# Row factors of eleven RMS norms: from a column of sums to a full-width product

## The chip, the cores and the metric

The kernel runs on one core of one Trainium2 chip. A core has a matrix engine (PE, TensorE), a vector engine (DVE), an activation engine (ACT), a slower general engine (POOL) and a queue that issues DMAs (SP). The engines run side by side, each takes its own instructions in order, and they wait for each other by semaphores. On-chip memory has 128 partitions; PE adds up its products in eight PSUM banks of 128x512 fp32.

The metric is the device time of one launch in microseconds (us). Lower is better. Runs of the kernel before: 2305.17, 2305.32 and 2305.44 us, median 2305.32.

## The reference, cut to what matters

Two layers over 512 tokens of width 1024. Each layer has four residual steps, and each step begins with a norm over the features of a token:

```python
def rmsnorm(x, g):
    xf = x.astype(jnp.float32)
    y = xf * lax.rsqrt(jnp.mean(xf * xf, axis=-1, keepdims=True) + RMS_EPS)
    return (y * g.astype(jnp.float32)).astype(x.dtype)

def swiglu(x, w_gu, w_down):
    g, u = jnp.split(x @ w_gu, 2, axis=-1)
    return (jax.nn.silu(g) * u) @ w_down

for i in range(DEPTH):                                            # DEPTH = 2
    h = h + 0.5 * swiglu(rmsnorm(h, ffn1_norm[i]), ...)
    hn = rmsnorm(h, mix_norm[i])
    h = h + (ssd_mixer(hn, ...) if i == 0 else neighbourhood_attention(hn, ...))
    h = h + 0.5 * swiglu(rmsnorm(h, ffn2_norm[i]), ...)
    gate = jax.nn.sigmoid(rmsnorm(h, ple_norm[i]) @ ple_w_gate[i])
    h = h + gate * rmsnorm(p[i] @ ple_w_proj[i], ple_post_norm[i])
```

The SSD mixer has one more norm, over its 2048 inner features, ahead of its output matrix. That makes eleven norms whose row factor, 1/sqrt(mean square + eps) of each token, is computed by the code that is changed here: two times (first FFN, mixer, second FFN, projection of `p`, gate), and the one inside the SSD. The norms of the attention's queries and keys have code of their own and stay.

## The kernel before, in words

**Layout and precision.** The stream `h` lies feature-major: eight tiles of 128 features by 512 tokens. A token is a column, so a norm's sum over features runs over the partitions and over the eight tiles. Nearly every matrix product is made of three fp32r products (fp32r is the rounded fp32 format that PE multiplies in one pass): high part by high part, high by low, low by high. Weights arrive by DMA as fp32 (`load_unit`), ACT casts them to the high part `wh` (L221, `split_raw`), DVE subtracts to get the low part `wl` (L223). There are three buffers of each, and `unit()` hands out the next pair. `gemm` issues the three products of every block (L278, L281, L282). In the FFNs most of the gate and up matrices run as a seven-product scheme over blocks with 256 columns (L508 to L510).

**The norm.** While a step writes `h`, it splits every tile by the norm's gain (L306, L307) and adds up squares: ACT squares (L328), POOL or, for the last tile, DVE adds into one 128x512 tile `acc` (L332). The products that follow run on the gained but unscaled tiles; the row factor is multiplied in where a result leaves PSUM, so it may come later than the first products. It is made in two steps:

- `begin`: PE sums `acc` over the partitions, four fp32 products with one column each (L346; every fp32 product stands as two records in the trace), so that the 512 sums lie as 128x4. DVE scales, adds eps (L349) and takes the inverse square root of the 128x4 tile by an integer seed and three Newton steps (`newton_rsqrt`, L313 to L319: eleven instructions).
- `end`: PE spreads the 128x4 factors to all partitions as 128x512, four fp32 products with the identity (L356), and ACT copies them from PSUM into a tile `rt` (L359).

`end` is written some products after `begin`. In an FFN the point for `begin` is `mid()`, inside the first pair of gate and up products; `end` comes after four blocks of the next product. In the SSD (`ssd`) `begin` follows the first product and `end` five blocks of the next; right behind `end`, DVE scales all eight tiles (L681, L687) and splits them (L304). In the attention (`keys`) and the gate (`ple`) the points lie in the same way within the first two or three products. After `begin`, an FFN calls `ahead(norm)`: the next four preparations of weights (sums and differences of weight blocks, L243 to L248, and splits), which on DVE are queued behind the instruction that the norm has left as `ss.last`.

**Order.** The kernel is written for a planner that follows the code's order as a priority, simulates the engines and issues on each engine the first instruction that is ready, so the order in the trace can differ from that of the code; `tc.issue_after` and `tc.keep_in_program_order` tie down single places. Tiles come from pools with a fixed number of buffers: `sq` (squares and their sum) 4, `rt` 3, PSUM banks `px` 3 and `mm` 5.

**Function tables.** ACT evaluates Silu, Tanh, Exp and Ln from a table that it has loaded; the trace shows each load as ACT_TABLE_LOAD. Casts, copies and squares run with whichever table is loaded. Before the change there are seven loads in the run.

Of the kernel before, what the change touches and what calls it, by code (L numbers as in the profile page):

```python
# [8 lines left out]
F32R = mybir.dt.float32r  # L9
I32 = mybir.dt.int32  # L10
AF = mybir.ActivationFunctionType
ALU = mybir.AluOpType
AX = mybir.AxisListType

P = 128
T = 512
D = 1024
# [8 lines left out]
EPS = 1e-6  # L26
NH = 32
NG = 8
NC = T // P
# [41 lines left out]
def trunk(ctx, tc, A, out):  # L71
    nc = tc.nc
    v, s, g, te, sy = nc.vector, nc.scalar, nc.gpsimd, nc.tensor, nc.sync


    cp = ctx.enter_context(tc.tile_pool(name="cp", bufs=1))
# [10 lines left out]
    def nm(t):  # L87
        uid[0] += 1
        return f"{t}{uid[0]}"

    def sm(shape, dt=F32):
        return sp.tile([P] + list(shape), dt, name=nm("sm"), tag="sm", bufs=12)

    def slot(tag, bufs):
        return lambda dt=F32: bp.tile([P, T], dt, name=nm(tag), tag=tag, bufs=bufs)

    hs, t2, sc, sq = slot("hs", 8), slot("t2", 7), slot("sc", 15), slot("sq", 4)

    def md(dt=F32):
        return bp.tile([P, 2, T], dt, name=nm("md"), tag="md", bufs=24)  # L100
# [4 lines left out]
    def rt():  # L105
        return bp.tile([P, T], F32, name=nm("rt"), tag="rt", bufs=3)

    def bank(tag, bufs):
        return ps.tile([P, T], F32, name=nm("ps"), tag=tag, bufs=bufs)

    mm_bank = lambda: bank("mm", 5)
    px_bank = lambda: bank("px", 3)
# [4 lines left out]
    msk = cp.tile([P, M_N], F32, name="msk")  # L117
    ones_d = cp.tile([P, P], F32, name="ones_d")
    v.memset(ones_d, 1.0 / D)

    idle = ps.tile([P, T], F32, name="idle", tag="px", bufs=3)
    for _ in range(14):
# [2 lines left out]
    ident = msk[:, M_ID:M_ID + P]  # L125
# [16 lines left out]
    stop = A.get("stage", 4 * DEPTH)  # L142
# [168 lines left out]
    def newton_rsqrt(m, y, a):  # L311

        v.tensor_scalar(out=y.bitcast(I32), in0=m.bitcast(I32), scalar1=1, scalar2=None, op0=ALU.arith_shift_right)  # L313
        v.tensor_scalar(out=y.bitcast(I32), in0=y.bitcast(I32), scalar1=-1, scalar2=0x5F3759DF,
                        op0=ALU.mult, op1=ALU.add)
        for _ in range(3):
            v.tensor_mul(out=a, in0=y, in1=y)
            v.scalar_tensor_tensor(out=a, in0=a, scalar=-0.5, in1=m, op0=ALU.mult, op1=ALU.mult)
            last = v.scalar_tensor_tensor(out=y, in0=a, scalar=1.5, in1=y, op0=ALU.add, op1=ALU.mult)  # L319
        return last  # L320

    class SumSq:
# [8 lines left out]
            else:  # L331
                (v if fast else g).tensor_add(out=self.acc, in0=self.acc, in1=q)  # L332

        def rsqrt(self, scale=1.0, eps=EPS):
            pt = px_bank()
            te.matmul(out=pt, lhsT=ones_d, rhs=self.acc, start=True, stop=True)
            m, a, y = sc(), sc(), rt()
            v.tensor_scalar(out=m, in0=pt, scalar1=scale, scalar2=eps, op0=ALU.mult, op1=ALU.add)
            newton_rsqrt(m, y, a)
            return y  # L340

        def begin(self, scale=1.0, eps=EPS):

            pt = px_bank()
            for c in range(NC):
                te.matmul(out=pt[:, c:c + 1], lhsT=self.acc[:, c * P:(c + 1) * P], rhs=ones_d[:, :1],  # L346
                          start=True, stop=True)
            m, a, self.y = sm([NC]), sm([NC]), sm([NC])
            v.tensor_scalar(out=m, in0=pt[:, :NC], scalar1=scale, scalar2=eps, op0=ALU.mult, op1=ALU.add)  # L349
            self.last = newton_rsqrt(m, self.y, a)  # L350

        def end(self):

            pt = px_bank()
            for c in range(NC):
                te.matmul(out=pt[:, c * P:(c + 1) * P], lhsT=self.y[:, c:c + 1].to_broadcast([P, P]), rhs=ident,  # L356
                          start=True, stop=True)
            r = rt()
            s.copy(out=r, in_=pt)  # L359
            return r  # L360

    class Norm:

# [13 lines left out]

        def count(self, k, fast=False):
            self.ss.add(h[k], fast=fast or k == KD - 1)

        def factor(self):
            return self.ss.rsqrt()

        def begin(self, half=False):
            if half:
# [1065 lines left out]
    for i in range(stop):  # L1451
        l, w = divmod(i, 4)
        last = i == stop - 1
        m = None if last else Norm(gains[i + 1], (lambda: md(F32R)) if w == 2 else xa)
# [112 lines left out]
```

## Time and profile before

| | us |
|---|---|
| median of 3 runs | 2305.32 |
| the profiled execution | 2305.77 |
| its span, first to last instruction | 2304.0 |
| PE busy in it | 2292.0 |
| DVE busy in it | 1826.6 |
| ACT busy in it | 1179.0 |
| POOL busy in it | 323.7 |
| mean granted clock of PE | 1.000 |

All times in the profile are of one execution, counted from the first instruction. A row of the order of time gives start and duration in us, engine, line, operation, tile written and tiles read, and how often; in brackets stands the idle time of the engine ahead of it and what ended it. A matmul's duration reaches to its modelled end, and matmuls overlap; what one costs is read from the starts of its neighbours. A row of groups ends in busy time and mean ns of one, then the idle time ahead of the group. A row of waits reads: who waited, for whom, us in total, times, longest. A row of the chain is start, duration, what.

### The profile page before, as it was taken

The page shows a single profiled execution, that of the slowest core. Times are in us where ns is not written, and L with a number is a line of the kernel's source. Part 1 is how long each engine was busy: PE and PEld are TensorE (multiplying, and loading weights), DVE is VectorE, ACT ScalarE, POOL GpSimd, SP SyncE. Part 2 cuts the span into 40 slices and gives each one's busy share as a digit, 9 for nine tenths or more (in the row PEclk, how much of TensorE's full clock was granted, in tenths as well). Part 3 has the DMA queues.
Part 4 walks back from the last instruction along what each step waited for, and adds up shares of the span by engine and source line. Part 5 has one row for each costly group of instructions (what it writes and reads, how often), then busy time and mean ns, then how long its engine had stood idle before and what let it go on. Part 6 is the DMA issues. An engine that isn't in the chain of part 4 may idle for free.

```text
span 2304.0 us, 35426 instructions
## 1 busy us (share of the span) xinstructions
PE 2292.0 (99%) x13732; PEld 2025.5 (88%) x13732; DVE 1826.6 (79%) x2621; ACT 1179.0 (51%) x2038; POOL 323.7 (14%) x261
## 2 busy tenths in 40 slices
PE   9999999999999999999999999999999999999999
PEld 8899998888888888999998889999878888999987
DVE  7878878888788958987885897787578859887866
ACT  5433445877676864444445444444446745444452
POOL 0000001355555641000003100000110010000020
PEclk9999999999999999999999999999999999999999
DMA  5323323444444543333223233232557732333222
GB/s 185 116 83 106 110 73 130 164 155 138 146 140 151 188 158 119 106 101 106 94 78 104 101 102 107 84 102 83 165 183 220 219 119 83 111 106 101 87 92 73
DMA packets 105224, 281.69 MB, mean 122 GB/s; under 512 B 13136, under 2 KB 14032, under 8 KB 105056
## 3 DMA queue, kind: packets, MB, share of 16 engines
q1 hardware_dynamic: 104768, 279.30, 37.0%
q8 instruction: 107, 1.75, 0.3%
q14 instruction: 61, 0.50, 0.1%
q10 hardware_dynamic: 288, 0.14, 0.0%
HBM read 259.70 MB, written 13.40 MB: 119 GB/s over the span
## 4 chain that ended last, share of the span: by engine, by line
PE 95%; DVE 3%; DMA 1%; ACT 1%; issue 0%; SPq 0%; POOL 0%; ACTq 0%; POOLq 0%
PE ps L278 19%; PE ps L282 19%; PE ps L281 19%; PE ps L510 10%; PE ps L509 10%; PE ps L508 10%; PE ps L930 1%; PE ps L889 1%; PE ps L910 1%; PE ps L1325 1%; PE ps L1271 1%; DVE wl L223 1%; PE ps L845 1%; PE ps L834 1%; DVE md L304 1%; PE ps L1314 0%
## 5 line engine op out<-in xcount | busy, mean ns | idle before, releaser
L278 PE MATMUL ps<-md,wh 128*128 128x512 f32 (+1 forms) x2032 | 798.6, 393 | 0.0
L282 PE MATMUL ps<-md,wl 128*128 128x512 f32 (+1 forms) x2032 | 790.5, 389 | 1.6 <-DVE wl L223 1.6
L281 PE MATMUL ps<-md,wh 128*128 128x512 f32 (+1 forms) x2032 | 791.2, 389 | 0.0
L221 ACT CAST wh<-wr 128x1024 fp32r<-128x1024 f32 (+2 forms) x395 | 351.8, 892 | 500.9 <-PE ps L281 260.1
L223 DVE TENSOR_TENSOR wl<-wr,wh 128x1024 fp32r<-128x1024 f32 (+2 forms) x395 | 418.5, 1061 | 84.4 <-ACT wh L221 82.6
L282 PEld LDWEIGHTS ps<-md,wl 128*128 128x128 f32 x2032 | 381.5, 188 | 83.5 <-DVE wl L223 2.9
L278 PEld LDWEIGHTS ps<-md,wh 128*128 128x128 f32 x2032 | 382.2, 188 | 73.8 <-issue 0.7
L281 PEld LDWEIGHTS ps<-md,wh 128*128 128x128 f32 x2032 | 382.4, 188 | 71.5
L221 ACT CAST wh<-md 128x1024 fp32r<-128x1024 f32 x175 | 183.6, 1049 | 322.6 <-PE ps L509 296.1
L332 POOL TENSOR_TENSOR sq<-sq,sq 128x512 f32<-128x512 f32 x71 | 101.0, 1422 | 1637.7 <-ACT sq L328 1633.3
L510 PE MATMUL ps<-sc,wl 128*128 128x256 f32 x980 | 277.5, 283 | 0.8 <-DVE wl L223 0.8
L508 PE MATMUL ps<-sc,wh 128*128 128x256 f32 x980 | 276.9, 283 | 0.8 <-ACT wh L221 0.8
L509 PE MATMUL ps<-md,wh 128*128 128x256 f32 x980 | 277.4, 283 | 0.1
L510 PE MATMUL ps<-md,wl 128*128 128x256 f32 x980 | 277.3, 283 | 0.0
L509 PE MATMUL ps<-sc,wh 128*128 128x256 f32 x980 | 277.3, 283 | 0.0
L508 PE MATMUL ps<-md,wh 128*128 128x256 f32 x980 | 277.2, 283 | 0.0
L514 DVE TENSOR_TENSOR t<-ps,t 128x512 f32<-128x512 f32 x245 | 165.8, 689 | 137.6 <-PE ps L510 137.0
L223 DVE TENSOR_TENSOR wl<-md,wh 128x1024 fp32r<-128x1024 f32 x175 | 213.4, 1219 | 16.3 <-ACT wh L221 15.9
L508 PEld LDWEIGHTS ps<-sc,wh 128*128 128x128 f32 x980 | 187.7, 192 | 4.9 <-ACT wh L221 1.0
L509 PEld LDWEIGHTS ps<-sc,wh 128*128 128x128 f32 x980 | 187.7, 192 | 3.9
L509 PEld LDWEIGHTS ps<-md,wh 128*128 128x128 f32 x980 | 188.0, 192 | 1.6 <-DVE md L472 0.4
L508 PEld LDWEIGHTS ps<-md,wh 128*128 128x128 f32 x980 | 188.0, 192 | 1.3
(209 smaller groups left out, 2895.5 us busy)
## 6 DMA issues: line engine op xcount, KB each, us to landing
wr<-in_w_gw_dram SPq DMA_DIRECT2D x70, 512.0 KB, 3.5
md<-in_w_gw_dram SPq DMA_DIRECT2D x70, 512.0 KB, 5.0
wr<-in_w_in_dram SPq DMA_DIRECT2D x65, 512.0 KB, 3.5
wr<-in_w_dn_dram SPq DMA_DIRECT2D x128, 256.0 KB, 2.6
wr<-in_w_gu_dram SPq DMA_DIRECT2D x32, 512.0 KB, 3.5
hs<-crow SPq DMA_DIRECT2D x64, 256.0 KB, 3.7
wr<-in_w_dn_dram SPq DMA_DIRECT2D x32, 384.0 KB, 3.0
wr<-in_w_qkv_dram SPq DMA_DIRECT2D x24, 512.0 KB, 4.3
```

The lines of the kernel that those rows point to most:

```text
L221: splits.append(s.copy(out=hi[:, :n], in_=raw[:, :n]))
L223: v.tensor_sub(out=lo[:, :n], in0=raw[:, :n], in1=hi[:, :n])
L278: m = te.matmul(out=pt, lhsT=hi[:, sl], rhs=part(xp, 0, cols), start=first and k == 0, stop=False)
L281: te.matmul(out=pt, lhsT=hi[:, sl], rhs=part(xp, 1, cols), start=False, stop=False)
L282: gemm.last = te.matmul(out=pt, lhsT=lo[:, sl], rhs=part(xp, 0, cols), start=False, stop=last and k == n - 1)
L304: split.low = v.tensor_sub(out=dst[:, 1, :], in0=src, in1=dst[:, 0, :])
L332: (v if fast else g).tensor_add(out=self.acc, in0=self.acc, in1=q)
L508: te.matmul(out=o, lhsT=hi[:, sl], rhs=xh, start=j == 0 and kk == 0, stop=False)
L509: te.matmul(out=o, lhsT=hi[:, sl], rhs=xl, start=False, stop=False)
L510: te.matmul(out=o, lhsT=lo[:, sl], rhs=xh, start=False, stop=j == 1 and kk == 3)
L514: v.tensor_add(out=k[to], in0=pt, in1=k[other])
L834: te.transpose(out=pt[:, cs(i)], in_=src[:, cs(c)], identity=ident)
```

## The change

`begin` makes the factor for all partitions at once, and `end` only returns it. ACT casts the sum of squares to an fp32r high part; DVE takes the low part and adds eps, divided so that the sum over 128 partitions brings it to its value. PE multiplies both parts by a constant 128x128 matrix (`mean`, scale/1024 in every element), two products of 128x512, so each partition holds the mean square of every token. ACT takes the logarithm from PSUM, then exp(-0.5 x) as the seed, and its square; DVE does one Newton step in two instructions. The result is the `rt` tile itself. `ss.last`, behind which `ahead` queues, is now the instruction that makes the low part. The three constant matrices (scale 1, 4 and 0.5) are made once at the top of the kernel by three scalings on ACT. `SumSq.rsqrt` and `Norm.factor`, which nothing calls, are dropped.

```diff
     v.memset(ones_d, 1.0 / D)
+    mean = {}
+    for scale in (1.0, 4.0, 0.5):
+        mean[scale] = cp.tile([P, P], F32R, name=f"mean{len(mean)}")
+        s.mul(out=mean[scale], in_=ones_d, mul=scale)
...
         def begin(self, scale=1.0, eps=EPS):
 
+            hi, lo = sq(F32R), sq(F32R)
+            s.copy(out=hi, in_=self.acc)
+            self.last = v.scalar_tensor_tensor(out=lo, in0=self.acc, scalar=eps * D / (scale * P), in1=hi,
+                                               op0=ALU.add, op1=ALU.subtract)
             pt = px_bank()
-            for c in range(NC):
-                te.matmul(out=pt[:, c:c + 1], lhsT=self.acc[:, c * P:(c + 1) * P], rhs=ones_d[:, :1],
-                          start=True, stop=True)
-            m, a, self.y = sm([NC]), sm([NC]), sm([NC])
-            v.tensor_scalar(out=m, in0=pt[:, :NC], scalar1=scale, scalar2=eps, op0=ALU.mult, op1=ALU.add)
-            self.last = newton_rsqrt(m, self.y, a)
+            te.matmul(out=pt, lhsT=mean[scale], rhs=hi, start=True, stop=False)
+            te.matmul(out=pt, lhsT=mean[scale], rhs=lo, start=False, stop=True)
+            y, a = rt(), self.acc
+            s.activation(out=y, in_=pt, func=AF.Ln)
+            s.activation(out=y, in_=y, func=AF.Exp, scale=-0.5)
+            s.activation(out=a, in_=y, func=AF.Square)
+            v.scalar_tensor_tensor(out=a, in0=a, scalar=-0.5, in1=pt, op0=ALU.mult, op1=ALU.mult)
+            v.scalar_tensor_tensor(out=y, in0=a, scalar=1.5, in1=y, op0=ALU.add, op1=ALU.mult)
+            self.y = y
 
         def end(self):
-
-            pt = px_bank()
-            for c in range(NC):
-                te.matmul(out=pt[:, c * P:(c + 1) * P], lhsT=self.y[:, c:c + 1].to_broadcast([P, P]), rhs=ident,
-                          start=True, stop=True)
-            r = rt()
-            s.copy(out=r, in_=pt)
-            return r
+            return self.y
```

More of the change, by code (lines that the diff above doesn't have):

```diff
@@ L332, in add, with begin @@
                 (v if fast else g).tensor_add(out=self.acc, in0=self.acc, in1=q)
-        def rsqrt(self, scale=1.0, eps=EPS):
-            pt = px_bank()
[L336 to L342, printed above, removed]
-            pt = px_bank()
-            for c in range(NC):
-                te.matmul(out=pt[:, c:c + 1], lhsT=self.acc[:, c * P:(c + 1) * P], rhs=ones_d[:, :1],
-                          start=True, stop=True)
-            m, a, self.y = sm([NC]), sm([NC]), sm([NC])
-            v.tensor_scalar(out=m, in0=pt[:, :NC], scalar1=scale, scalar2=eps, op0=ALU.mult, op1=ALU.add)
-            self.last = newton_rsqrt(m, self.y, a)
-        def end(self):
-            pt = px_bank()
-            for c in range(NC):
-                te.matmul(out=pt[:, c * P:(c + 1) * P], lhsT=self.y[:, c:c + 1].to_broadcast([P, P]), rhs=ident,
-                          start=True, stop=True)
-            r = rt()
-            s.copy(out=r, in_=pt)
-            return r
+        def begin(self, scale=1.0, eps=EPS):
+            hi, lo = sq(F32R), sq(F32R)
+            s.copy(out=hi, in_=self.acc)
+            self.last = v.scalar_tensor_tensor(out=lo, in0=self.acc, scalar=eps * D / (scale * P), in1=hi,
+                                               op0=ALU.add, op1=ALU.subtract)
+            pt = px_bank()
+            te.matmul(out=pt, lhsT=mean[scale], rhs=hi, start=True, stop=False)
[7 more added lines that the diff above has]
+            self.y = y
+        def end(self):
+            return self.y
     class Norm:
@@ L379, in count @@
             self.ss.add(h[k], fast=fast or k == KD - 1)
-        def factor(self):
-            return self.ss.rsqrt()
         def begin(self, half=False):
```

## The prediction

> **What bounds the kernel now.** I read the page first, then the waits of all engines, then PE's order of time at one norm.
>
> ```profile
> PE 2292.0 (99%) x13732; PEld 2025.5 (88%) x13732; DVE 1826.6 (79%) x2621; ACT 1179.0 (51%) x2038; POOL 323.7 (14%) x261
> ...
> PE 95%; DVE 3%; DMA 1%; ACT 1%; issue 0%; SPq 0%; POOL 0%; ACTq 0%; POOLq 0%
> ```
>
> PE is busy in 2292.0 of 2304.0 us, and 95% of the chain that ended last is PE. A microsecond taken out of PE's queue shortens the run unless another engine then makes PE wait.
>
> ```profile
> ACT wh L221 <- PE ps L281: 282.2, 170, 5.3
> ...
> ACT rt L359 <- PE ps L356: 30.7, 7, 9.7
> ...
> DVE sm L349 <- PE ps L346: 27.6, 9, 6.9
> ```
>
> In the list of waits the others wait for PE: ACT stands 282.2 us ahead of the weight casts of L221 until PE gives a buffer back, so weights are normally ready well ahead. The last two rows are the norm: ACT waited 30.7 us for the spread factor, DVE 27.6 us for the sums.
>
> ```profile
> 2258.82 0.39 PE L282 MATMUL ps<-md,wl 128*128 128x512 f32 x1
> 2259.05 0.95 PE L346 MATMUL ps<-ones_d,sq 128*128 128x1 f32 x8
> ...
> 2260.18 0.40 PE L281 MATMUL ps<-md,wh 128*128 128x512 f32 x1
> ...
> 2265.21 0.39 PE L282 MATMUL ps<-md,wl 128*128 128x512 f32 x1
> 2265.44 1.05 PE L356 MATMUL ps<-msk,sm 128*128 128x128 f32 x8
> ...
> 2266.56 0.39 PE L281 MATMUL ps<-md,wh 128*128 128x512 f32 x1
> ```
>
> From 2260.18 to 2265.21 PE starts 22 wide matmuls, 5.03/22 = 0.229 us each; that pitch, not the 0.39, is what one costs. From 2258.82 to 2260.18 two wide ones and the sums start: 1.36 - 0.46 = 0.90 us for the sums of L346 with the hitch behind them. In the same way 1.35 - 0.46 = 0.89 us for the spreading of L356. **One norm costs PE 1.79 us.**
>
> **The change part by part.**
>
> ```profile
> L356 PE MATMUL ps<-msk,sm 128*128 128x128 f32 x88 | 12.0, 279 | 0.1
> L346 PE MATMUL ps<-ones_d,sq 128*128 128x1 f32 x88 | 10.4, 239 | 0.0
> ```
> ```profile
> 1678.26 1.84 PE ps L1183 x8
> ```
>
> *PE.* Eight records each and 88 in all make 11 norms. Both groups go. In their place come two 128x512 products of fp32r tiles; L1183, eight products of just that kind in 1.84 us, gives 0.23 each, 0.46 together. They hitch nothing, as they have the form of their neighbours. Saved: 1.79 - 0.46 = 1.33 us per norm, 14.7 us over 11.
>
> *DVE and ACT.* The prices:
>
> ```profile
> L780 ACT ACTIVATE t<-ps 128x512 f32<-128x512 f32 x16 | 9.3, 586 | 0.3 <-DVE md L760 0.3
> L328 ACT ACTIVATE sq<-md 128x512 f32<-128x512 f32 x16 | 10.1, 633 | 1.2
> ```
> ```profile
> L571 DVE SCALAR_TENSOR_TENSOR hs<-ps,hs 128x512 f32<-128x512 f32 x160 | 109.8, 686 | 56.7 <-PE ps L282 56.7
> ```
> ```profile
> 30.18 0.16 DVE L349 TENSOR_SCALAR sm<-ps 128x4 f32<-128x4 f32 x1 [3.42 <-PE ps L346]
> ...
> 32.36 0.16 DVE L319 SCALAR_TENSOR_TENSOR sm<-sm,sm 128x4 f32<-128x4 f32 x1
> ...
> 35.98 0.69 DVE L440 TENSOR_TENSOR t<-ps,rt 128x512 f32<-128x512 f32 x1
> ```
>
> DVE loses 12 tiny instructions that held it from 30.18 to 32.52, 2.34 us, and gets three wide ones at 0.69: 2.07, so 0.27 us less. ACT loses the copy (0.59, below) and gets a cast (0.63), Ln from PSUM (0.59), Exp and Square (0.63 each): 1.89 us more. Then the function tables:
>
> ```profile
> 408.54 1.28 ACT L729 ACT_TABLE_LOAD   x1
> 409.84 0.42 ACT L729 ACTIVATE md<-md 128x256 f32<-128x256 f32 x1
> 410.27 1.28 ACT L759 ACT_TABLE_LOAD   x1
> 411.57 0.63 ACT L759 ACTIVATE t<-t 128x512 f32<-128x512 f32 x1
> ```
>
> L729 is the one Ln there is: it loads a table, and Tanh behind it loads another. From load to activation takes 1.30 us. Whether Exp right behind Ln loads again no row shows. I take the dearer end, a load for Ln and one for Exp, 2.60 us per norm, as Tanh reloaded at once; the cheap end is one load. ACT's sum is about 4.5 us a norm, 49 us in all, on an engine busy 1179.0 us: hidden behind PE, as long as the weight casts keep their lead.
>
> The Trainium skill (ScalarE: Activation LUTs, What ACT_TABLE_LOAD costs) gives about 2.66 us for a switch with its drain. The rows above show 1.30, so the measurement decides; by the page the two tight norms below would each lose 2.7 us more, and the forecast would be 2298.3.
>
> *Order and new waits.* ACT's cast waits for the last add of the squares, the low part on DVE for the cast, PE's products for both, Ln on ACT for PE, the two Newton steps on DVE for Square. Behind ACT's Ln stand weight casts and Silu; but the copy of L359 stood there before. The factor no longer passes through PE, so it isn't tied to the matmul at which `end` was written. In the first FFN the products end 0.35 sooner than L346 did, so Ln can start at 29.83, and 0.59 + 1.30 + 1.26 + two steps 1.37 give 34.35 for the factor, where its first reader began at 35.98: 1.6 us sooner, more than PE's gain, so this norm keeps its 1.33.
>
> Two norms have little room. The one ahead of the SSD:
>
> ```profile
> 361.31 0.68 DVE L332 TENSOR_TENSOR sq<-sq,sq 128x512 f32<-128x512 f32 x1
> ...
> 369.14 0.68 DVE L681 TENSOR_TENSOR t<-ps,rt 64x512 f32<-64x512 f32 x1 [1.87 <-ACT rt L359]
> ...
> 398.61 1.22 DVE L223 TENSOR_TENSOR wl<-wr,wh 128x1024 fp32r<-128x1024 f32 x1
> ```
> ```profile
> 362.94 1.05 ACT L221 CAST wh<-wr 128x1024 fp32r<-128x1024 f32 x1 [0.50 <-ACT ea L659]
> 368.52 0.59 ACT L359 COPY rt<-ps 128x512 f32<-128x512 f32 x1 [4.53 <-PE ps L356]
> ```
> ```profile
> 398.87 0.39 PE L281 MATMUL ps<-md,wh 128*128 128x512 f32 x1
> 399.88 0.50 PE L282 MATMUL ps<-md,wl 128*128 128x512 f32 x1 [0.62 <-DVE wl L223]
> ```
>
> The squares are complete at 361.99, ACT is free from 362.44. Cast to 363.07, low part to 363.76, products to 364.2. ACT meanwhile casts weights (1.05, to 364.12), loads for Ln (365.42), Ln (366.01), loads for Exp (367.31), Exp and Square (368.57), then 1.37 on DVE: 369.94, 0.8 us after the 369.14 of now. From there DVE works without a pause until PE waits for L223 at 398.87. PE would be there 1.33 us sooner and DVE 0.8 later, so the wait grows by 2.1 and this norm nets a **loss of 0.8**. With one load, and the weight cast behind Ln, it is 2.35 us better and gains the full 1.33: those are its bounds. I take the loss, from the loads taken above.
>
> The norm ahead of the second layer's first FFN:
>
> ```profile
> 1307.76 0.68 DVE L332 TENSOR_TENSOR sq<-sq,sq 128x512 f32<-128x512 f32 x1
> ...
> 1318.07 0.68 DVE L440 TENSOR_TENSOR t<-ps,rt 128x512 f32<-128x512 f32 x1
> ```
> ```profile
> 1308.60 1.99 ACT L221 CAST wh<-wr 128x1024 fp32r<-128x1024 f32 x2 [1.02 <-issue]
> ```
>
> Squares at 1308.44, cast to 1309.07, two weight casts to 1311.06, load 1312.36, Ln 1312.95, load 1314.25, Exp and Square 1315.51, two steps 1316.9: 1.2 us ahead of 1318.07, since the preparations that `ahead` queues on DVE now lie in the wait for Square. Gain 1.2.
>
> *Buffers.* The two parts of the squares and the running sum hold three of the four `sq` tiles, the sum's PSUM bank is held until the first Newton step. Where the projection's norm begins while the next one counts squares, all four are taken, and the next square waits until the products are through, about 1 us, in a sum that is not due for many matmuls: nothing.
>
> *The start.*
>
> ```profile
> 0.73 0.41 ACTq L1397 DMA_DIRECT2D cst<-in_cst_dram  x1
> 1.00 0.17 DVE L661 MEMSET ones_t<- 128x128 f32 x1
> 4.12 0.72 ACT L306 ACTIVATE md<-hs,cst 128x512 fp32r<-128x512 f32 x1 [1.46 <-DMA cst<-in_cst_dram]
> 7.33 0.72 ACT L306 ACTIVATE md<-hs,cst 128x512 fp32r<-128x512 f32 x1 [1.46 <-DMA hs<-in_x_dram]
> ```
>
> Three scalings stand ahead of ACT's load of `cst`. L661, far down in the code, ran at 1.00: the planner issues what is ready, and the load is ready when the scalings still wait for the memset. So nothing; the other bound is 2.2 us (third rival). The deleted `rsqrt` and `factor` have no row: nothing. The 1.5 KB of constants move other tiles' addresses; no row prices that, and I take nothing.
>
> **Sum.** Nine norms at 1.33 are 12.0, plus 1.2, minus 0.8: 12.4 us. The profiled execution took 2305.77 us, 0.45 above the median of the runs; 2305.77 - 12.4 = 2293.4, and from the median 2305.32: **2292.9 us.**
>
> **The rivals.**
>
> *DVE-fed norms keep nothing.* The first FFN, the SSD, the second layer's FFN and the attention read their factor in stretches where DVE or ACT feeds PE. If DVE is late there by as much as PE is early, seven norms count: 7 x 1.33 = 9.3, less 0.8: 2296.8. For it speaks the wait at 398.87; against it the earlier factors above.
>
> *One load for Ln and Exp.* The factor then comes 1.3 us sooner, the SSD's norm gains 0.5 and the FFN's its full 1.33: 10 x 1.33 + 0.5 = 13.8, **2291.5**. No Exp runs behind the Ln at 409.84 to decide it. The Trainium skill (ScalarE: Activation LUTs, Table sets: the hidden batching unit) names a set that holds both, which is this rival.
>
> *The head waits.* If the scalings go first, with a load (1.30 from 1.17) and at most 0.63 each, `cst` is asked for as late as 4.4 and read 3.4 later, at 7.8 instead of 4.12. Of these 3.7 us the pause of 1.46 before 7.33 hides its part: +2.2, 2295.1.
>
> *Casts come late (slower).* ACT's block at a norm is 0.63 + 2.60 + 0.59 + 1.26 = 5.1 us without a weight cast. A unit of 24 matmuls lasts PE 5.5 us; less a cast (1.05) and its difference on DVE (1.22) one unit covers 3.2. With only one unit ready, PE would wait 1.9 us a norm; 11 x 1.9 = 20.9 against 14.7 saved: 2311.5. It decides where the cover is under 5.1 - 1.3 = 3.8 us. Against it: the 282.2 us that ACT waits for free buffers show more than one unit ready.
>
> *No effect.* PE's savings are all given back as waits elsewhere in a new order of the planner: 2305.
>
> **How the numbers follow.** Chances: forecast 0.58, DVE-fed 0.14, one load 0.08, head 0.05, late casts 0.09, no effect 0.06. About 0.2%, 4.6 us, is what a measurement can tell from no change here. Faster 0.85, within 0.06, slower 0.09. The low end takes all 14.7, the 0.9 us wait at 398.87 with its restart gone and DVE's 0.27 x 11 = 3.0: 2286.7. The high end takes the DVE-fed case with the late head and 1 us more: 2300. That holds four cases and leaves out the last two.
>
> **What would show it.** Right: PE's order of time shows two wide products at 0.23 and nothing where L356 stood; its busy time drops some 15 us; the factor comes sooner in ten norms and later ahead of the SSD, with a longer wait near 398; two table loads a norm. Wrong: new PE waits for weight parts within 10 us of the norms, a first product later than 6.6, or PE pauses ahead of the new products.

## The result, and the profile after

The changed kernel took **2300.3 us** (median of 18 runs, 2299.86 to 2302.04), the kernel before 2305.25 beside it (18 runs): a ratio of 0.9979, 95% interval 0.9972 to 0.9987. The gain is 4.95 us, where 12.4 were forecast; the profiled execution took 2300.35 us. Faster, then, but by less than half.

The page of the changed kernel, its span and the busy time of each engine (before: PE 2292.0 of 2304.0, DVE 1826.6, ACT 1179.0):

```profile
span 2298.5 us, 35082 instructions
PE 2280.6 (99%) x13578; PEld 2008.7 (87%) x13578; DVE 1829.9 (80%) x2522; ACT 1228.2 (53%) x2098; POOL 322.2 (14%) x261
```

PE is busy 11.4 us less, but it stands 2298.5 - 2280.6 = 17.9 us where it stood 12.0: 5.9 us of the saving came back as waits. ACT's extra 49.2 us come to the 49 of the forecast. The groups of ACT, the loads of the norms and of the Silu alone (busy time, mean ns):

```profile
L348 ACT ACT_TABLE_LOAD x11 | 14.1, 1283 | 0.2
L349 ACT ACT_TABLE_LOAD x11 | 14.1, 1283 | 0.2
L434 ACT ACT_TABLE_LOAD x4 | 5.1, 1283 | 0.1
```

Two loads a norm, as taken; and four at L434, the Silu behind an FFN's norm, where the kernel before had two: the norm's loads throw the Silu's table out. These two further loads, 2.6 us of ACT, were not in the forecast. PE's order of time in the changed kernel at the last gate, where L346 and L356 stood before:

```profile
2254.97 0.39 PE L345 MATMUL ps<-sq,mean 128*128 128x512 f32 x1
2255.20 0.40 PE L346 MATMUL ps<-sq,mean 128*128 128x512 f32 x1
2255.43 0.40 PE L282 MATMUL ps<-md,wh 128*128 128x512 f32 x1
```

2255.43 - 2254.97 = 0.46 us for the two products, the price that was put in. The waits of PE (who waited, for whom, total, times, longest):

```profile
PE ps L286 <- DVE wl L227: 3.1, 3, 1.2
PE ps L346 <- DVE sq L342: 2.1, 5, 0.7
PE ps L282 <- DVE t L749: 1.6, 1, 1.6
...
PE ps L345 <- ACT sq L341: 0.6, 1, 0.6
```

The second and fourth are stands ahead of the new products themselves. The first is for low weight parts, at 380, 398 and 1332, the first two behind the norm ahead of the SSD. The third is new and lies in the SSD's steps, the stretch in which the SSD's convolutions and state steps run.

**Where it went.** The table compares the start of one and the same PE product in two traces: the changed kernel's start minus that of before, at the end of each stretch, less that at its beginning (the products of the norms are left out of the count). Each cell is the time that PE gained (-) or lost (+) in the stretch. "No tables", "one load" and "combined" are experiments below. One load and combined have the same code in the first stretch and still differ by 1.1 us there, so that stretch is not read closer than about 1 us.

| stretch, us of before | norm in it | forecast | changed | no tables | one load | combined |
|---|---|---|---|---|---|---|
| 0 to 59.6 | first FFN | -1.33 | -2.39 | -3.25 | -2.69 | -1.59 |
| to 403.6 | ahead of the SSD | +0.8 | +0.96 | -1.43 | -0.41 | -0.40 |
| to 437.5 | none | 0 | +1.82 | +3.04 | +1.70 | +0.01 |
| to 896.7 | inside the SSD | -1.33 | -1.60 | -1.63 | -0.80 | -0.67 |
| to 950.3 | second FFN | -1.33 | +0.33 | -1.28 | -1.28 | -1.28 |
| to 1256.6 | projection | -1.33 | -0.31 | -0.33 | -0.30 | -1.38 |
| to 1303.8 | gate | -1.33 | -1.07 | -1.37 | -1.37 | -1.37 |
| to 1356.9 | 2nd layer, first FFN | -1.2 | +1.05 | -1.63 | -0.78 | -0.95 |
| to 1900.0 | attention | -1.33 | -1.52 | -1.64 | -1.56 | -0.74 |
| to 2226.3 | second FFN | -1.33 | -1.03 | -1.28 | -1.28 | -1.28 |
| to 2298.4 | projection and gate | -2.66 | -1.70 | -1.66 | -1.70 | -2.75 |
| sum | | -12.4 | -5.46 | -12.46 | -10.47 | -12.40 |

The stretches that lose 1 us or more against the forecast are the SSD's steps, which have no norm (1.8), two FFNs (1.7 and 2.3) and each projection (1.0, the second by the last row). The first FFN is off the other way, by 1.1: a wait of 0.99 us for a low part that PE had at 54.9 before is gone. The rows of three of these places:

*The FFN at 899.* Last weight product ahead of the norm and the two new ones, PE's order of time of the changed kernel; in brackets the idle time and what ended it:

```profile
899.07 0.39 PE L286 MATMUL ps<-md,wl 128*128 128x512 f32 x1
900.07 0.50 PE L345 MATMUL ps<-sq,mean 128*128 128x512 f32 x1 [0.61 <-ACT sq L341]
900.79 0.50 PE L346 MATMUL ps<-sq,mean 128*128 128x512 f32 x1 [0.22 <-DVE sq L342]
```

The squares are late here, because from the factor inside the SSD on DVE is never held up by PE: it stops only five times for 0.79 us, each time for a product of ACT's that DVE's own result feeds (L306 before, L310 after), the same in both kernels. DVE's order of time, first reader of that factor and last add of the next squares, before and after:

```profile
859.59 0.69 DVE L1102 TENSOR_TENSOR t<-t,rt 128x512 f32<-128x512 f32 x1 [1.87 <-ACT rt L359]
...
898.55 0.68 DVE L332 TENSOR_TENSOR sq<-sq,sq 128x512 f32<-128x512 f32 x1
```
```profile
859.99 0.69 DVE L1095 TENSOR_TENSOR t<-t,rt 128x512 f32<-128x512 f32 x1
...
898.68 0.68 DVE L336 TENSOR_TENSOR sq<-sq,sq 128x512 f32<-128x512 f32 x1
```

39.0 us from the one to the other before, 38.7 after. So the squares come when the factor says; the factor is 0.4 us later, although PE is 1.2 us earlier, and PE waits for the difference at 899. The 0.4 us are what PE, and with it the sum of squares, had already lost by then, above all in the SSD's steps. From the complete sum (the end of POOL's last add, L332 before and L336 after) to the factor's first reader it takes 859.99 - 843.53 = 16.5 us, and 859.59 - 843.17 = 16.4 before: with its two loads the new way to the factor is no shorter than the old one through PE.

*The projection at 1233.* PE, the first new product, the one ahead of the second, and the second:

```profile
1232.56 0.50 PE L345 MATMUL ps<-sq,mean 128*128 128x512 f32 x1
...
1233.12 0.39 PE L285 MATMUL ps<-md,wh 128*128 128x512 f32 x1
1234.22 0.50 PE L346 MATMUL ps<-sq,mean 128*128 128x512 f32 x1 [0.71 <-DVE sq L342]
```

From 1233.12 a pitch of 0.23 would give 1233.35; it is 1234.22, 0.87 us more. The high part was in time here; the low part was not, and POOL and DVE show what it stood behind:

```profile
1232.14 1.30 POOL L336 TENSOR_TENSOR sq<-sq,sq 128x512 f32<-128x512 f32 x1 [2.78 <-ACT sq L332]
```
```profile
1233.47 0.69 DVE L342 SCALAR_TENSOR_TENSOR sq<-sq,sq 128x512 fp32r<-128x512 f32 x1 [1.18 <-POOL sq L336]
```

POOL's add is the next norm's: the projection's own sum was complete by 1222.0. The four `sq` tiles are then the projection's sum, the gate norm's sum, its running square and the high part; the low part starts when POOL's add has freed the running square, at 1232.14 + 1.30 = 1233.44. It is the same at 2231. In the other norms the low part follows the cast at once (900.05 behind 899.40 + 0.62). That the tile is the cause is read from these rows; no run had a fifth one.

*The SSD's steps.* ACT's order of time around 408, before and after, and a wait of PE after (L735 before is L728 after, the exponential of a row; L729 is L722, the logarithm):

```profile
408.02 0.50 ACT L735 ACTIVATE sc<-ps 128x256 f32<-128x256 f32 x1
```
```profile
406.56 1.28 ACT L722 ACT_TABLE_LOAD   x1
...
408.55 1.28 ACT L728 ACT_TABLE_LOAD   x1
409.85 0.38 ACT L728 ACTIVATE sc<-ps 128x256 f32<-128x256 f32 x1
```
```profile
430.91 0.47 PE L282 MATMUL ps<-md,wh 128*128 128x512 f32 x1 [1.59 <-DVE t L749]
```

The code of this place is the same in both. The planner turned the order round: the logarithm's load now runs ahead of the exponential, which has to load again and comes 1.8 us later on a clock on which PE is 1.4 us earlier. From that row SP issues 16 small DMAs, and 21 us further on PE waits 1.59 us.

### The profile page after: what moved, and what is told of

Its sections match the earlier page's. It is cut to its first block, busy times and chain, and to the rows that moved or that the text cites. A ratio compares the mean times of both kernels' runs of the same rounds, so it can differ in the third digit from the quotient of the medians.

```text
span 2298.5 us, 35082 instructions
## 1 busy us (share of the span) xinstructions
PE 2280.6 (99%) x13578; PEld 2008.7 (87%) x13578; DVE 1829.9 (80%) x2522; ACT 1228.2 (53%) x2098; POOL 322.2 (14%) x261
## 4 chain that ended last, share of the span: by engine, by line
PE 89%; DVE 6%; ACT 2%; issue 1%; DMA 1%; SPq 0%; POOL 0%; DVEq 0%; POOLq 0%; ACTq 0%
PE ps L282 17%; PE ps L286 17%; PE ps L285 17%; PE ps L503 10%; PE ps L502 10%; PE ps L501 10%; DVE wl L227 1%; PE ps L923 1%; PE ps L882 1%; PE ps L1264 1%; PE ps L903 1%; PE ps L1318 1%; PE ps L838 1%; PE ps L827 1%; ACT wh L225 1%
## 5 line engine op out<-in xcount | busy, mean ns | idle before, releaser
L336 POOL TENSOR_TENSOR sq<-sq,sq 128x512 f32<-128x512 f32 x71 | 98.9, 1393 | 1635.2 <-ACT sq L332 1315.6
```

## The experiments

Each time is the median beside the kernel before on the same chip, which took 2305.16 (no tables, one load, one fp32 sum, the SSD's norm as before), 2305.48 (the release alone, the row, late products, the three together), 2305.43 (the fp32 product alone, constants) and 2305.68 (the release in the kernel before).

**No tables.** Logarithm and exponential become two scaled copies of the same size, so the kernel leaves both functions out.

```diff
-            s.activation(out=y, in_=pt, func=AF.Ln)
-            s.activation(out=y, in_=y, func=AF.Exp, scale=-0.5)
+            s.activation(out=y, in_=pt, func=AF.Copy, scale=1e-4)
+            s.activation(out=y, in_=y, func=AF.Copy, scale=0.5)
```

> Ln and Exp are replaced by two scaled copies of the same tile and size, so no table is loaded for a norm; the logarithm and the exponential are left out and the factor is not an inverse root. Theory TABLES (the two loads between the products and the factor make the factor late and hold weight casts back): the waits that the changed kernel has behind the norms go, above all the 4.4 us at three places behind the SSD's norm and 1.3 us near 1331, so about 5 us less than the changed kernel's 2300.3: 2295. Theory QUEUE (PE stands ahead of the new products because the cast and the low part come after the last square): nothing of its 4.7 us goes, 2299.5 or more.

Measured 2292.9 (ratio 0.9947, 0.9932 to 0.9962): 7.4 us below the changed kernel, with the same products, casts and Newton step. PE at the same FFN:

```profile
897.25 0.39 PE L345 MATMUL ps<-sq,mean 128*128 128x512 f32 x1
897.48 0.40 PE L346 MATMUL ps<-sq,mean 128*128 128x512 f32 x1
```

No stand: the squares are in time again. DVE's first reader of the factor inside the SSD:

```profile
855.39 0.69 DVE L1095 TENSOR_TENSOR t<-t,rt 128x512 f32<-128x512 f32 x1
```

From the complete sum there to this reader it takes 855.39 - 841.47 = 13.9 us, 2.5 less than with the two loads. The table shows the gain in the stretches of the SSD's norm (2.4 us) and of the FFNs (1.6 and 2.7). The waits for low parts at 380, 398 and 1332 are gone, as TABLES had it; the third place behind the SSD's norm that it named, the one at 431, is not: PE waits 1.95 us there, and the SSD's steps lose 3.0, 1.2 more than with the tables. The projections keep their loss.

**One load.** Behind the cast, the set that holds both functions is loaded by name.

```diff
-            s.copy(out=hi, in_=self.acc)
+            cast = s.copy(out=hi, in_=self.acc)
+            with tc.issue_after(cast.ins):
+                s.preload_act_table_set("natural_log_exp_and_others")
```

> One load of a table that holds Ln and Exp, issued right behind the cast, in place of two loads; all else as in the changed kernel. TABLES: the factor comes 1.3 us sooner and the load no longer stands between products and Ln, so some 60% of what leaving the loads out brings: 2297. QUEUE: within 0.8 us of 2300.3.

Measured 2295.5 (0.996, 0.9946 to 0.9975). ACT at the norm ahead of the SSD, with the changed kernel's rows behind it:

```profile
360.28 1.28 ACT L343 ACT_TABLE_LOAD   x1
...
362.53 0.59 ACT L350 ACTIVATE rt<-ps 128x512 f32<-128x512 f32 x1
363.15 0.64 ACT L351 ACTIVATE rt<-rt 128x512 f32<-128x512 f32 x1
```
```profile
361.58 1.28 ACT L348 ACT_TABLE_LOAD   x1
362.87 0.60 ACT L348 ACTIVATE rt<-ps 128x512 f32<-128x512 f32 x1
363.49 1.28 ACT L349 ACT_TABLE_LOAD   x1
```

One load, and it lies beside the low part and the products, where ACT had nothing to do for the norm. The edit does two things, one load fewer and the other moved ahead, and together they are worth 2300.3 - 2295.5 = 4.8 us, 0.44 us a norm; which of the two brings how much is not parted. The loads that are left cost 2295.5 - 2292.9 = 2.6 us in that place, 0.24 us a norm, against 1.28 that each holds ACT.

**One fp32 sum.** A single fp32 product takes the place of cast, low part and two products, and `ahead` is held behind the last Newton step.

```diff
-            te.matmul(out=pt, lhsT=mean[scale], rhs=hi, start=True, stop=False)
-            te.matmul(out=pt, lhsT=mean[scale], rhs=lo, start=False, stop=True)
+            te.matmul(out=pt, lhsT=mean[scale], rhs=self.acc, start=True, stop=True)
...
-            v.scalar_tensor_tensor(out=y, in0=a, scalar=1.5, in1=y, op0=ALU.add, op1=ALU.mult)
+            self.last = v.scalar_tensor_tensor(out=y, in0=a, scalar=1.5, in1=y, op0=ALU.add, op1=ALU.mult)
```

> No cast and no low part: PE multiplies the fp32 sum of squares by the constant matrix in fp32, one product instead of two; eps, 1e-6, is left out; what is prepared ahead is queued behind the last Newton step. QUEUE: the waits at the products (4.7 us in the changed kernel) go. An fp32 product stands as two records; if each takes 0.23 us, PE pays as much as now and the time is 2295.6; if they take 0.46 each, 0.46 x 11 = 5.1 us come back and the time is 2300.7, but the waits at the products are gone in the trace all the same. TABLES: the waits behind the norms stay.

Measured 2313.6 (1.0036, 1.0023 to 1.0049). Neither number holds: 13.3 us slower than the changed kernel. The edit had moved two things, and the next two runs part them.

**The release alone.** The changed kernel with the one line of `last` moved.

```diff
-            self.last = v.scalar_tensor_tensor(out=lo, in0=self.acc, ...
+            v.scalar_tensor_tensor(out=lo, in0=self.acc, ...
...
-            v.scalar_tensor_tensor(out=y, in0=a, scalar=1.5, in1=y, op0=ALU.add, op1=ALU.mult)
+            self.last = v.scalar_tensor_tensor(out=y, in0=a, scalar=1.5, in1=y, op0=ALU.add, op1=ALU.mult)
```

> The changed kernel, with the preparations that `ahead` queues on DVE held back behind the last Newton step instead of the low part; nothing is left out. Theory RELEASE (the early release of these preparations, right behind the low part, is worth several us, and its loss is what made the fp32-sum run slow): 2305 to 2313, with waits of PE for the low weight parts of the kind that the fp32-sum run shows (7.3 us). Theory PRODUCT (that run was slow only through its fp32 product, 0.9 us instead of 0.46, and what this did to the order): within 1 us of the changed kernel, 2299.3 to 2301.3.

Measured 2315.9 (1.0045, 1.0031 to 1.0059): 15.6 us for one line. DVE's order of time in the first FFN, here and in the changed kernel:

```profile
33.44 0.69 DVE L351 SCALAR_TENSOR_TENSOR sq<-sq,ps 128x512 f32<-128x512 f32 x1 [3.83 <-ACT sq L350]
...
34.77 1.22 DVE L247 TENSOR_TENSOR md<-wr,md 128x1024 f32<-128x1024 f32 x1
```
```profile
27.25 1.22 DVE L247 TENSOR_TENSOR md<-wr,md 128x1024 f32<-128x1024 f32 x1
...
33.03 0.69 DVE L351 SCALAR_TENSOR_TENSOR sq<-sq,ps 128x512 f32<-128x512 f32 x1 [2.17 <-ACT sq L350]
```

DVE stands 3.83 us with the preparations queued behind the factor. They come 7.5 us later (34.77 against 27.25), of which 2.3 are squares that were late in this execution, and are then in the way of everything else. By the starts of PE's products 6.9 us are lost in the first stretch and 2.6 to 2.7 in each of the other three with an FFN's norm: RELEASE holds in kind, though the time is 2.9 us above its range. PE pays at 53, in the order of time and in windows of the same kernel (busy time of each engine, then PE's granted clock, DMA share, GB/s):

```profile
53.12 0.40 PE L285 MATMUL ps<-md,wh 128*128 128x512 f32 x1
56.77 0.79 PE L286 MATMUL ps<-md,wl 128*128 128x512 f32 x1 [3.25 <-DVE wl L227]
57.36 0.63 PE L282 MATMUL ps<-md,wh 128*128 128x512 f32 x1
57.78 0.63 PE L285 MATMUL ps<-md,wh 128*128 128x512 f32 x1
```
```profile
57.00:62.00 5.00, 5.00 (x12) 3.89 (x13) 5.00 (x9) 2.20 (x3) 0.00 (x0) 0.50 0.67 202
```

**The fp32 product alone**, with `ahead` queued behind the last add, so that nothing holds the preparations.

```diff
-                (v if fast else g).tensor_add(out=self.acc, in0=self.acc, in1=q)
+                self.last = (v if fast else g).tensor_add(out=self.acc, in0=self.acc, in1=q)
...
+            te.matmul(out=pt, lhsT=mean[scale], rhs=self.acc, start=True, stop=True)
```

> The changed kernel with one fp32 product of the whole sum of squares in place of cast, low part and two fp32r products (eps is left out, so a row's factor lacks it), but with the preparations of `ahead` queued behind the last add of the squares, so that nothing holds them back. The fp32-sum run before it took 2313.6 us and differed in two things at once. Theory RELEASE (the late release did all the harm): the fp32 product costs PE about 0.44 us a norm more, 11 x 0.44 = 4.8 us, and gives back the waits ahead of the two products and 1.3 us ahead of each factor, some 4 us: 2299 to 2302. Rival PRODUCT (the fp32 product itself costs far more than its records show): 2307 or more.

Measured 2297.9 (0.9968, 0.9955 to 0.998), below the range that RELEASE gave and 2.4 us faster than the changed kernel. PE at the FFN, and ACT in the SSD's steps:

```profile
898.24 1.11 PE L341 MATMUL ps<-sq,mean 128*128 128x512 f32 x2
...
899.41 0.39 PE L285 MATMUL ps<-md,wh 128*128 128x512 f32 x1
```
```profile
406.72 0.50 ACT L723 ACTIVATE sc<-ps 128x256 f32<-128x256 f32 x1
```

One product of the usual form starts between the two rows of PE, so 899.41 - 898.24 - 0.23 = 0.94 us for the fp32 sum, 0.48 more than the two fp32r products, 5.3 us over eleven. The stands ahead of the products are gone, but that is not what makes the run faster than the changed kernel. By the starts of PE's products it gains 2.0 us on it in the SSD's steps, where the row (L723) runs ahead of the logarithm as it did before the change, and 0.6 in all other stretches together. So the fp32 product about pays for itself by the stands that it spares; and as the preparations are also released a little sooner here, at the last add, this run does not part the two.

**The release in the kernel before.** The early release, behind the last add as in the run before, with the narrow norm as it was.

```diff
-                (v if fast else g).tensor_add(out=self.acc, in0=self.acc, in1=q)
+                self.last = (v if fast else g).tensor_add(out=self.acc, in0=self.acc, in1=q)
...
-            self.last = newton_rsqrt(m, self.y, a)
+            newton_rsqrt(m, self.y, a)
```

> The kernel before with one thing of the change alone: what `ahead` prepares is queued on DVE behind the last add of the squares, no longer behind the eleven small instructions of the inverse square root; the narrow norm itself is as before. It tells how much of the change's gain is the earlier release and how much the two wide products. Theory PRODUCTS (before, the release came only some 3 to 6 us later and the weight parts were still in time but for the 1.15 us wait at 53.5): 2304 to 2305.5. Theory RELEASE (the earlier release is worth as much to the old form as to the new): 2300 or less; the small instructions then stand behind 1.2 us wide ones and the factor comes later, which could also make it slower than 2306.

Measured 2309.0 (1.0013, 1.0004 to 1.0023): slightly slower, by 3.3 us. The waits of PE name a place, the second layer's first FFN, which loses 1.5 us in the profiled execution (at 2307.33 the fastest of the ten, so about half of the loss is not in this trace):

```profile
PE ps L356 <- DVE sm L319: 3.1, 1, 3.1
```

In the narrow form the factor goes back through PE, whose queue stands at L356 while DVE prepares weights. So the early release is no gain in the narrow form. That the wide form can use it because nothing on PE's queue waits for the factor fits both runs, but is argued.

**The SSD's norm as before, the other ten changed.** A list names the norms that keep the narrow form; the rest of the narrow code stands as before.

```diff
+NARROW = (1,)
...
+            if self.which in NARROW:
+                return self.narrow_begin(scale, eps)
```

> The norm ahead of the SSD alone is made as before (narrow sums, DVE, spreading); the other ten as changed. If that norm is where the most is lost (3.3 us of new waits between 378 and 431 and 0.6 at its products, against 1.3 saved on PE), the time is 2300.3 - 2.6 = 2297.7. If those waits come from another order of the SSD's work and not from this factor, it is 2300.3 + 1.3 = 2301.6.

Measured 2298.8 (0.9972, 0.9961 to 0.9983), 1.5 us below the changed kernel. By the starts of PE's products it loses 0.02 and 0.11 us in the second and third stretch, where the changed kernel loses 0.96 and 1.82. So the norm ahead of the SSD is a net loss in its changed form, as forecast, and the turned order in the steps hangs on it too. The two stretches give 2.6 us, the 2297.7 of the expectation; the median has 1.5 of it.

**The row ahead of the logarithm.**

```diff
-            s.activation(out=dtk[:, :, 64:], in_=dtk[:, :, 64:], func=AF.Ln)
...
-            s.activation(out=rowt[:, 256:], in_=pr[:, :256], func=AF.Exp)
+            row_exp = s.activation(out=rowt[:, 256:], in_=pr[:, :256], func=AF.Exp)
+            with tc.issue_after(row_exp.ins):
+                s.activation(out=dtk[:, :, 64:], in_=dtk[:, :, 64:], func=AF.Ln)
```

> The changed kernel with one order tied down on ACT in the SSD's steps: the logarithm on the state steps stands behind the row's exponential, as the kernel before had them, so that the row's 16 DMAs are issued some 2 us sooner. Theory FLIP (the 1.75 us that PE waits near 429, and which the kernel before doesn't have, comes from the logarithm's table load that slid ahead of the row): that wait goes and the time is 2298.5. Rival (the wait comes from DVE, 0.8 us late from the norm on): the wait stays at 1.5 us or more and the time is 2300.3 within 0.6.

Measured 2298.9 (0.9974, 0.9964 to 0.9983). ACT and PE of this run:

```profile
406.81 0.49 ACT L727 ACTIVATE sc<-ps 128x256 f32<-128x256 f32 x1
```
```profile
429.30 0.47 PE L282 MATMUL ps<-md,wh 128*128 128x512 f32 x1
```

The row's exponential comes 3 us sooner, the wait at 429 is gone and the third stretch loses 0.03 instead of 1.82: FLIP holds. Of the links between the row's DMAs and the DVE instruction that PE waited for, none was taken away by itself.

**Late products for the projections.** Cast and low part stay at `begin`, the products are written at `end`.

```diff
+            self.parts = scale, hi, lo
+            if not late:
+                self.root()
...
         def finish():
+            ss.root()
             r3 = ss.end()
...
-        yield pp, (lambda: ss.begin(4.0, 4.0 * EPS)), finish
+        yield pp, (lambda: ss.begin(4.0, 4.0 * EPS, True)), finish
```

> The changed kernel, but in the two norms of the projections the two wide products are written where `end` stands instead of right behind the cast and the low part; the other nine norms are as changed. Theory WAIT (PE stands about 1.0 us in each of the two ahead of the second product, because cast and low part need 1.4 us behind the last add and the products are written right there): 2298.2, no pause of PE near 1233 and 2231. Rival (the stand is absorbed by a later wait): 2300.3 within 0.6.

Measured 2299.1 (0.9972, 0.9961 to 0.9983). PE in the first projection:

```profile
1238.15 0.39 PE L351 MATMUL ps<-sq,mean 128*128 128x512 f32 x1
1238.38 0.40 PE L352 MATMUL ps<-sq,mean 128*128 128x512 f32 x1
```

The pause is gone, and the two projections are 1.0 us better, each by itself (first: -1.37 instead of -0.31). The gates behind them give 0.2 and 0.5 back; 1.2 of the 2.1 arrived. The run does not tell a late cast from a missing tile, since the products now stand behind both.

**The three together**: one load, the row, the late products.

> One table load a norm (set loaded behind the cast), the row ahead of the logarithm, and the late products of the two projections, all three. If the three add up: 2295.5 - 1.75 - 2.1 = 2291.7. If one load already freed the time near 429 or at the projections: 2293.5 to 2295.5.

```diff
+            cast = s.copy(out=hi, in_=self.acc)
+            with tc.issue_after(cast.ins):
+                s.preload_act_table_set("natural_log_exp_and_others")
...
+            with tc.issue_after(row_exp.ins):
...
+            ss.root()
```

Measured **2292.2** (five runs, 2290.7 to 2293.38; 0.9941, 0.9929 to 0.9954). It beats both kernels, the changed one by 8.1 us. It lies 0.5 above the sum that was expected, and 0.7 below the sum of the three gains as measured (4.8, 1.4 and 1.2). Its page:

```profile
span 2291.6 us, 35075 instructions
PE 2277.9 (99%) x13578; PEld 2009.3 (88%) x13578; DVE 1831.1 (80%) x2522; ACT 1218.1 (53%) x2090; POOL 323.6 (14%) x261
```

PE's busy time is 14.1 us under that of before, and it stands 13.7 us where it stood 12.0.

**Constants alone.** The kernel before with the three scalings and their matrices, used by nothing; all eleven norms are narrow.

```diff
+    for scale in (1.0, 4.0, 0.5):
+        mean[scale] = cp.tile([P, P], F32R, name=f"mean{len(mean)}")
+        s.mul(out=mean[scale], in_=ones_d, mul=scale)
```

> The kernel before, with the three constant matrices and their scalings on ACT added and used by nothing, so that start and addresses are those of the change; all eleven norms are as before. The forecast priced both at nothing: 2305.3 within 1 us. Rival (the scalings or the moved addresses cost something that the change then paid): 2306.5 or more.

Measured 2305.65 against 2305.43 (1.0001, 0.9991 to 1.001). Start and moved addresses cost nothing, as priced, and the rival of the late head falls with it.

## Why the prediction was right in kind and wrong in size

- *PE saves 1.33 a norm.* Right. The products cost 0.46 where they don't wait, and in the combined kernel five stretches gain 1.28 to 1.38 per norm. The sign that busy PE "drops some 15 us" came to 11.4 in the changed kernel and 14.1 in the combined one.
- *ACT's 4.5 us a norm are "hidden behind PE, as long as the weight casts keep their lead".* **This is the step that failed.** The size of ACT's work was right (49), two loads were taken, and their place was worked out in three norms; in the other eight they were costed at nothing. By the run without tables they cost 7.4 us in all. The 282.2 us of waiting that I read as lead is a sum over the run; the price falls in the stretches that DVE and ACT feed, where a late factor (859.99) is a late square (898.68) is a waiting PE (900.07). Ten factors were to come sooner; the one inside the SSD came later. A cover has to be shown per norm, and I had shown it for three.
- *"ACT's cast waits for the last add, the low part for the cast, PE's products for both."* Written down and costed at nothing: the second error. The list of waits has 0.6 + 2.1 = 2.7 us ahead of the products, which the prediction itself had named as a sign of being wrong. 1.4 of them are the two projections and belong to the next point. In the other 1.3, L346 before needed only the last add, so the same place in PE's queue was too early: at 899 the last add ends at 898.68 + 0.68, the second product starts at 900.79, 1.43 us behind it. The 0.8 us of standing there needs both, the late square of the point above and the cast and low part behind it; without tables it is gone.
- *Buffers: "all four are taken, and the next square waits", in a sum that is not due: nothing.* The third error. All four were taken, but the next square already had its tile, and the low part waited for it, with PE behind it: DVE 1.18 and PE 0.71 us at 1233, the same at 2231, and each projection gains 0.3 where 1.33 were forecast.
- *The norm ahead of the SSD loses 0.8.* Right in size: +0.96. Squares were complete at 359.60 and the factor was there at 367.52, 7.92 us; before 361.99 and 369.11, 7.12: 0.8 later, the worked sum to a tenth. The longer wait near 398 came as two, 0.92 at 380.14 and 1.17 at 398.40, against 0.62 before. With one load the stretch gains 0.41, near the 0.5 of that rival and not the full 1.33 that was named as the bound; without loads it gains 1.43.

```profile
358.92 0.68 DVE L336 TENSOR_TENSOR sq<-sq,sq 128x512 f32<-128x512 f32 x1
...
366.83 0.69 DVE L352 SCALAR_TENSOR_TENSOR rt<-sq,rt 128x512 f32<-128x512 f32 x1
```

- *The second layer's first FFN gains 1.2.* Wrong: it loses 1.05, and gains 1.63 without tables. I had followed its factor, and that is sooner: 1315.81 - 1307.22 = 8.6 us behind the complete squares, where 8.5 were worked out and the kernel before took 9.6. I had not followed what ACT's two loads and the Silu's third do to the casts behind; the runs show only that the loss is gone when all three are (no tables), and that with one load, named and moved ahead, the stretch gains 0.78.
- *A new order elsewhere.* Not in the sum at all: the planner's new order at 406 cost 1.8 us in a stretch without a norm. The rival "no effect" named such a thing as a whole; as a term of its own it had no price. The norms' loads are not its cause: without tables the order is turned as well.
- *The early release.* I used it in one place ("now lie in the wait for Square"). It carries far more than that: without it the change would be 10.4 us slower than the kernel before.
- *The rivals.* "DVE-fed" (2296.8) has the right mechanism for the SSD and the FFN behind it, but not for attention (-1.52) and the first FFN (-2.39). "One load" put 1.4 us on the second load; with that load gone and the other moved ahead it is 4.8. "Late casts" names the waits for low parts (3.1 us by the list, its kind), a seventh of its 20.9. The Trainium skill (ScalarE: Activation LUTs, What ACT_TABLE_LOAD costs) has 1283 ns for a load and a drain on top: the load agrees to the ns with the groups above, and from load to activation is 1.29 (361.58 to 362.87), so no drain shows.

That the forecast of 2292.9 is the time of the run without tables is chance: without loads, the same working would have given all 14.7 us. That run gained 12.5 by its trace, because it loses 5 us against the working in the SSD's steps and the projections, and gains 1.9 more in the first FFN than its 1.33.

## What to carry to other kernels

Cover is a property of a place, not of an engine's busy share: for each of the places where work moves to ACT, look for the first reader of the result and for what paces the engine that feeds PE there. When a sum goes from "needs the last add" to "needs the last add, a cast and a low part", the products have to move down PE's queue by as much, or the queue waits. Two tiles more from a pool can put the wait on the new work itself: ask who holds each tile at that moment. And if a chain grows longer on one engine, look at what is queued behind its end on the others: one line that releases the preparations earlier was worth three times the change itself.

## What the runs showed of the hardware that was not expected

- **A long stand costs twice.** After PE stood from 53.12 to 56.77 in the run with the late release, its granted clock was 0.50 from 57 to 62 and one product cost 0.43 us (57.36 to 57.78) instead of 0.23: about 2.3 us more (5 us, of which 0.20/0.43 is lost) for a stand of 3.4. Finer windows have 0.84 for 55 to 56, 0.50 for 56 to 57 and 0.75 for 62 to 63, so the clock was down from about 55.7 to 62.5. A milder case is a window of the run on the row, in the attention, at a granted clock of 0.64, after two stands of 0.31 and 1.15 us (up to 1744.55 and to 1746.35). Its profiled execution lost 2.8 us on the changed kernel there, waits and clock together, which its median (2298.9, the profiled one 2301.57) does not show.

```profile
1748.00:1752.00 4.00, 4.00 (x17) 3.49 (x16) 3.56 (x10) 2.15 (x4) 0.00 (x0) 0.64 1.03 293
```

  The Trainium skill (TensorE: Matmul & The Clock Gate, Part 1: The HAM clock gate) says that PE falls to half its clock after an idle window of about 3.4 us; the 0.50 agrees. The length does not: here the clock fell some 2.2 us after the last product had ended (53.12 + 0.40), and in the attention after stands of 1.5 us in all.
- **Logarithm and exponential are two loads unless the set is named.** The Trainium skill (ScalarE: Activation LUTs, Table sets: the hidden batching unit) counts one load for Ln and then Exp. The changed kernel loads 22 times for eleven pairs; with the set named there are 11 loads for them, at L343.
- **A wide fp32 product costs 0.94 us** of PE's queue (898.24 to 899.41), twice the two fp32r products of the same width. Here the stands that it spares about pay for it.
